# Sum of absolute differences by row: longer loads on one queue, the second half of y in the first half's place, and the absolute sums on ScalarE

## The chip, the cores and the metric

The kernel runs on one core of a Trainium2 chip (trn2). The metric is the device time of one execution in microseconds (us). Lower is better.

## The reference

`x` and `y` are float32 matrices of 1024 rows and 4096 columns. The result is one float32 number per row:

```python
def reference(x, y, axis):            # axis = -1
    return np.sum(np.abs(x - y), axis=axis).astype(np.float32)
```

Two matrices of 16.78 MB each are read, 33.55 MB in all, and 4 KB are written.

## The kernel before

The 128 partitions of the on-chip memory (SBUF) each take K = 8 neighbouring rows: partition p holds rows 8p to 8p + 7 (`"(p k) c -> p k c"`, L15 to L17). So one pass of the loop (L29) handles one row of every partition, a tile of 128 x 4096 elements with 16 KB per partition, 2 MB in all. There are eight passes, and each has four steps:

- L33: SyncE's queue (SP) loads the row of x into the tile `tx`;
- L34: ScalarE's queue (ACTq) loads the row of y into the tile `ty`;
- L35: VectorE subtracts, `tx = tx - ty`, in place;
- L36: VectorE sums the absolute values of `tx` along the row into one column of `ro` (128 x 8).

After the loop SP stores `ro` (L38). ScalarE itself computes nothing; it only issues the loads of y.

`tx` and `ty` come from two pools of four buffers each (L23, L24). The first four passes therefore find free buffers, and a later load has to wait until its buffer has been read: the load of x for the reduction of four passes before, the load of y for the subtraction. The loads are written in program order, but the order of the operations on each engine is set by the framework's scheduler, not by the order in the source: the trace shows which order it chose. All waits (semaphores) are put in by the framework.

Of the kernel before, what the change touches and what calls it, by code (L numbers as in the profile page):

```python
# [5 lines left out]

KCS = [1]*8

@with_exitstack
def kernel(ctx, tc, x, y, axis, out):  # L10
    nc = tc.nc
    P = nc.NUM_PARTITIONS
    R, C = x.shape
    K = R // P
    xr = x.rearrange("(p k) c -> p k c", p=P, k=K)  # L15
    yr = y.rearrange("(p k) c -> p k c", p=P, k=K)
    orr = out.rearrange("(p k) -> p k", p=P, k=K)  # L17
    kcs = KCS
    assert sum(kcs) == K
    pools = {}  # L20
    for kc in set(kcs):
        pools[kc] = (
            ctx.enter_context(tc.tile_pool(name=f"px{kc}", bufs=4)),  # L23
            ctx.enter_context(tc.tile_pool(name=f"py{kc}", bufs=4)),  # L24
        )
    with tc.tile_pool(name="pr", bufs=1) as poolr:
        ro = poolr.tile([P, K], mybir.dt.float32)
        o = 0
        for kc in kcs:  # L29
            poolx, pooly = pools[kc]  # L30
            tx = poolx.tile([P, kc, C], x.dtype)
            ty = pooly.tile([P, kc, C], y.dtype)
            nc.sync.dma_start(out=tx, in_=xr[:, o:o+kc, :])  # L33
            nc.scalar.dma_start(out=ty, in_=yr[:, o:o+kc, :])  # L34
            nc.vector.tensor_sub(out=tx, in0=tx, in1=ty)  # L35
            nc.vector.reduce_sum(out=ro[:, o:o+kc], in_=tx, axis=mybir.AxisListType.X, apply_absolute_value=True)  # L36
            o += kc
        nc.sync.dma_start(out=orr, in_=ro)  # L38


# [1 line left out]
_INS = ['x', 'y', 'axis']  # L42
_OUTS = [((1024,), 'float32')]
#: Inputs that are plain numbers.
_NUMBERS = {'axis': -1}


def kernel(**inputs):
    import numpy as _np
    import concourse.bacc as _bacc  # L50
    import concourse.tile as _tile
    from concourse import mybir as _mybir
    from concourse.bass_utils import run_bass_kernel_spmd as _run

    nc = _bacc.Bacc("TRN2", target_bir_lowering=False, num_devices=1)  # L55
    arrays, args = {}, []
    for name in _INS:
        if name in _NUMBERS:
            args.append(_NUMBERS[name])
            continue  # L60
        a = _np.ascontiguousarray(inputs[name])
        if a.dtype.kind in "iu":
            a = a.astype(_np.int64)
        arrays[f"in_{name}_dram"] = a
        args.append(nc.dram_tensor(f"in_{name}_dram", a.shape, _mybir.dt.from_np(a.dtype), kind="ExternalInput").ap())
    for i, (shape, dtype) in enumerate(_OUTS):
        dt = _mybir.dt.from_np(_np.dtype(dtype))
        args.append(nc.dram_tensor(f"out_{i}_dram", shape, dt, kind="ExternalOutput").ap())
    with _tile.TileContext(nc) as tc:
        kernel(tc, *args)  # L70
    r = _run(nc, [arrays], core_ids=[0])
    got = tuple(r.results[0][f"out_{i}_dram"] for i in range(len(_OUTS)))
    return got[0]
```

## Time and profile before

| | |
|---|---|
| time, median of 3 runs | 97.6 us (97.56 to 97.62) |
| span of the profiled execution, first to last instruction | 95.8 us |
| VectorE (DVE) busy | 69.9 us, 73% of the span, 16 operations |
| ScalarE, TensorE, GpSimd | nothing, but for four small constants written by GpSimd |
| loads | 33.55 MB, mean 350 GB/s over the span |
| chain that ended last | DMA 68%, DVE 24%, issue 4%, ACTq 1% |

The runs give the time of an execution as a whole and the profile gives the span inside one, so the 1.8 us between 97.6 and 95.8 are what lies around the span. For the profiled execution no time but its span is shown.

How to read it: the page gives for each engine its busy time as a share of the span, and a strip of 40 equal slices of the span with the busy tenths in each. The chain is the work that ended last, followed backwards from the last instruction, at each step to whatever released it. A group of instructions is one line of the source on one engine: the tiles it writes and reads, the shapes, how often, the busy time, the mean of one, and the idle time just before it with what ended that. For a queue, the page gives the packets and bytes that it moved and the time that its packets took as a share of 16 transfer engines over the whole span. SPq and ACTq are the parts of SyncE and ScalarE that issue transfers.

### The profile page before, as it was taken

How to read it: one execution, taken by the hardware profiler on the slowest of the kernel's cores; microseconds unless marked ns; L12 is line 12 of the kernel's file. 1: busy time of each engine (PE TensorE's matmuls, PEld its weight loads, DVE VectorE, ACT ScalarE, POOL GpSimd, SP SyncE). 2: the span in 40 equal slices, each digit the busy share in tenths (PEclk: the TensorE clock that was granted, in tenths of full speed). 3: DMA queues.
4: the chain of work that ended last, by engine and by line, in shares of the span. 5: the costliest groups of instructions: out<-in, count | busy, mean ns of one | idle time of the engine just before them, and what ended most of it. 6: DMA issues, size and time to landing. Idle time of an engine off the chain costs nothing.

```text
span 95.8 us, 95 instructions
## 1 busy us (share of the span) xinstructions
DVE 69.9 (73%) x16; POOL 0.2 (0%) x4
## 2 busy tenths in 40 slices
DVE  0000069996930499999982999999909999999990
POOL 0000000000000000000000000000000000000000
DMA  4899999999999999999999999999999995000000
GB/s 109 369 431 424 424 438 438 438 431 438 431 424 438 424 417 431 431 411 431 438 438 424 431 431 431 424 424 424 431 411 438 438 438 212 0 0 0 0 0 2
DMA packets 2448, 33.56 MB, mean 350 GB/s; under 512 B 400, under 2 KB 400, under 8 KB 400
## 3 DMA queue, kind: packets, MB, share of 16 engines
q1 hardware_dynamic: 1296, 16.78, 41.7%
q10 hardware_dynamic: 1152, 16.78, 41.1%
HBM read 33.55 MB, written 0.00 MB: 350 GB/s over the span
## 4 chain that ended last, share of the span: by engine, by line
DMA 68%; DVE 24%; issue 4%; ACTq 1%
DMA ty<-in_y_dram 68%; DVE tx L35 14%; DVE ro L36 10%; ACTq L34 1%
## 5 line engine op out<-in xcount | busy, mean ns | idle before, releaser
L35 DVE TENSOR_TENSOR tx<-tx,ty 128x4096 f32<-128x4096 f32 x8 | 35.4, 4422 | 23.6 <-DMA ty<-in_y_dram 23.6
L36 DVE TENSOR_REDUCE ro<-tx 128x1 f32<-128x4096 f32 x8 | 35.1, 4413 | 0.1
L55 POOL MEMSET const-bfloat16-1.0<- 128x1 bf16 x1 | 0.1, 103 | 0.0
L55 POOL MEMSET const-uint8-127<- 128x1 uint8 x1 | 0.1, 103 | 0.0
L55 POOL MEMSET const-float32-1.0<- 128x1 f32 x1 | 0.1, 100 | 0.0
L55 POOL MEMSET const-float32-0.0<- 128x1 f32 x1 | 0.1, 99 | 0.2 <-issue 0.2
## 6 DMA issues: line engine op xcount, KB each, us to landing
ty<-in_y_dram ACTq DMA_DIRECT2D x8, 2048.0 KB, 33.1
tx<-in_x_dram SPq DMA_DIRECT2D x8, 2048.0 KB, 23.6
out_dram<-ro SPq DMA_DIRECT2D x1, 4.0 KB, 1.4
```

Source lines behind the costliest of these rows:

```text
L34: nc.scalar.dma_start(out=ty, in_=yr[:, o:o+kc, :])
L35: nc.vector.tensor_sub(out=tx, in0=tx, in1=ty)
L36: nc.vector.reduce_sum(out=ro[:, o:o+kc], in_=tx, axis=mybir.AxisListType.X, apply_absolute_value=True)
L55: nc = _bacc.Bacc("TRN2", target_bir_lowering=False, num_devices=1)
```

## The change

The program now works with four large tiles instead of the pools. `xa` holds the first four rows of x of each partition, `xb` the last four, and `yb` the four rows of y that are needed now; `last` is a small tile for the end. The order of instructions on each engine is that of the source (`tc.manual_schedule()`).

- All loads are issued by SP, on one queue. The first four rows of x and then of y are one load each, 64 KB per partition; then follow three rows of x (48 KB per partition).
- After the subtraction of row k of the first half, row 4 + k of y is loaded into the place of row k of y. For the last row, x and y come in four pieces of 2304, 1152, 512 and 128 columns, x and y in turn.
- VectorE only subtracts. ScalarE takes the absolute value and the sum along the row in one operation (`activation` with `accum_out`).
- The last row is worked off piece by piece. ScalarE writes the sums of the first three pieces into three columns of `last`; VectorE writes the difference of the fourth piece beside them and sums the absolute values of these 3 + 128 columns into the last column of `ro`.

```diff
-KCS = [1]*8
+F32 = mybir.dt.float32
+ABS = mybir.ActivationFunctionType.Abs
+AX = mybir.AxisListType.X
+
+PIECES = [2304, 1152, 512, 128]
...
+    n_part = len(PIECES) - 1
+    H = K // 2
+    ps = ctx.enter_context(tc.tile_pool(name="ps", bufs=1))
+    with tc.manual_schedule():
+        xa = ps.tile([P, H, C], F32, tag="xa")
+        xb = ps.tile([P, H, C], F32, tag="xb")
+
+        yb = ps.tile([P, H, C], F32, tag="yb")
+        ro = ps.tile([P, K], F32, tag="ro")
+
+        last = ps.tile([P, n_part + PIECES[-1]], F32, tag="last")
+        nc.sync.dma_start(out=xa, in_=xr[:, 0:H, :])
+        nc.sync.dma_start(out=yb, in_=yr[:, 0:H, :])
+        nc.sync.dma_start(out=xb[:, 0:H - 1, :], in_=xr[:, H:K - 1, :])
+
+        def whole(tx, ty, k):
+            nc.vector.tensor_sub(out=tx, in0=tx, in1=ty)
+            nc.scalar.activation(tx, tx, ABS, accum_out=ro[:, k:k + 1])
+
+        for k in range(H):
+            whole(xa[:, k, :], yb[:, k, :], k)
+            if k < H - 1:
+                nc.sync.dma_start(out=yb[:, k, :], in_=yr[:, H + k, :])
+                continue
+            o = 0
+            for w in PIECES:
+                nc.sync.dma_start(out=xb[:, k, o:o + w], in_=xr[:, K - 1, o:o + w])
+                nc.sync.dma_start(out=yb[:, k, o:o + w], in_=yr[:, K - 1, o:o + w])
+                o += w
+        for k in range(H - 1):
+            whole(xb[:, k, :], yb[:, k, :], H + k)
+        tx, ty = xb[:, H - 1, :], yb[:, H - 1, :]
         o = 0
...
-            nc.sync.dma_start(out=tx, in_=xr[:, o:o+kc, :])
-            nc.scalar.dma_start(out=ty, in_=yr[:, o:o+kc, :])
-            nc.vector.tensor_sub(out=tx, in0=tx, in1=ty)
-            nc.vector.reduce_sum(out=ro[:, o:o+kc], in_=tx, axis=mybir.AxisListType.X, apply_absolute_value=True)
-            o += kc
+        for i, w in enumerate(PIECES):
+            s = slice(o, o + w)
+            if i < n_part:
+                nc.vector.tensor_sub(out=tx[:, s], in0=tx[:, s], in1=ty[:, s])
+                nc.scalar.activation(tx[:, s], tx[:, s], ABS, accum_out=last[:, i:i + 1])
+            else:
+                nc.vector.tensor_sub(out=last[:, n_part:n_part + w], in0=tx[:, s], in1=ty[:, s])
+                nc.vector.reduce_sum(out=ro[:, K - 1:K], in_=last, axis=AX, apply_absolute_value=True)
+            o += w
         nc.sync.dma_start(out=orr, in_=ro)
```

## Rows read from the trace of the kernel before

**Rows 1.** The page: the span, VectorE's busy time, and the transfers' share in 40 slices.

```profile
span 95.8 us, 95 instructions
...
DVE 69.9 (73%) x16; POOL 0.2 (0%) x4
...
DMA  4899999999999999999999999999999995000000
```

**Rows 2.** The chain of waits in order of time, its end: start, length, what.

```profile
36.97 34.71 DMA ty<-in_y_dram
71.68 0.02 issue
71.70 4.43 DVE tx L35
76.13 5.22 DVE ro L36 x2
81.34 3.36 issue
84.70 4.43 DVE tx L35
89.13 0.02 issue
89.15 4.42 DVE ro L36
```

**Rows 3.** The timeline of VectorE: start, length, operation, and the idle time before it.

```profile
12.92 4.43 DVE L35 TENSOR_TENSOR tx<-tx,ty 128x4096 f32<-128x4096 f32 x1 [12.92 <-DMA ty<-in_y_dram]
...
22.72 4.43 DVE L35 TENSOR_TENSOR tx<-tx,ty 128x4096 f32<-128x4096 f32 x1 [0.92 <-DMA ty<-in_y_dram]
32.51 4.43 DVE L35 TENSOR_TENSOR tx<-tx,ty 128x4096 f32<-128x4096 f32 x1 [5.37 <-DMA ty<-in_y_dram]
36.86 8.74 DVE L36 TENSOR_REDUCE ro<-tx 128x1 f32<-128x4096 f32 x2
...
76.04 8.74 DVE L36 TENSOR_REDUCE ro<-tx 128x1 f32<-128x4096 f32 x2
```

**Rows 4.** Stretches: busy time of DVE and POOL, clock, DMA share, GB/s (six between 12.9 and 71.7).

```profile
12.90:22.70 9.80, 8.85 (x2) 0.00 (x0) 1.00 1.01 431
...
32.50:42.30 9.80, 9.79 (x3) 0.00 (x0) 1.00 1.01 428
...
80.50:81.00 0.50, 0.50 (x1) 0.00 (x0) 1.00 0.02 0
```

**Rows 5.** The page: the two load queues, packets, MB, share of 16 engines.

```profile
q1 hardware_dynamic: 1296, 16.78, 41.7%
q10 hardware_dynamic: 1152, 16.78, 41.1%
```

**Rows 6.** The loads' issues (ns, minimum, median, maximum), and stretches at the start.

```profile
L34 ACTq DMA_DIRECT2D ty<-in_y_dram x8: 334/364/649, 0.7 to 50.0; - x8
...
L33 SPq DMA_DIRECT2D tx<-in_x_dram x8: 327/352/510, 0.7 to 60.9; - x8
...
0.73 1.88 SPq L33 DMA_DIRECT2D tx<-in_x_dram  x4
...
1.00:1.50 0.50, 0.00 (x0) 0.00 (x0) 1.00 0.00 0
1.50:2.00 0.50, 0.00 (x0) 0.00 (x0) 1.00 2.30 524
```

**Rows 7.** The waits of SP's queue: us in total, times, longest.

```profile
SPq L33 <- DVE ro L36: 46.5, 4, 18.7
```

**Rows 8.** The page: groups of instructions; busy us, mean ns of one, idle before.

```profile
L35 DVE TENSOR_TENSOR tx<-tx,ty 128x4096 f32<-128x4096 f32 x8 | 35.4, 4422 | 23.6 <-DMA ty<-in_y_dram 23.6
L36 DVE TENSOR_REDUCE ro<-tx 128x1 f32<-128x4096 f32 x8 | 35.1, 4413 | 0.1
...
L55 POOL MEMSET const-float32-1.0<- 128x1 f32 x1 | 0.1, 100 | 0.0
```

**Rows 9.** The timeline at the end: the store.

```profile
93.60 0.35 SPq L38 DMA_DIRECT2D out_dram<-ro  x1
```

**Rows 10.** Stretches around three places where the queues go from one load to the next.

```profile
11.30:12.90 1.60, 0.00 (x0) 0.00 (x0) 1.00 1.06 451
21.00:22.60 1.60, 0.80 (x1) 0.00 (x0) 1.00 1.06 451
30.80:32.40 1.60, 0.00 (x0) 0.00 (x0) 1.00 1.07 451
```

15 lines of the change are left out of this document (1 added, 14 removed).

## The prediction

> **What bounds the kernel now.** I read the page first, then the chain of waits, then the work stage by stage, then VectorE's order of time. On the page VectorE is busy for 73% of the span and the transfers fill nine tenths of each slice from the third to the 33rd [rows 1]: neither is the bound throughout. The chain of waits tells them apart in time. Until 71.70 us it is the loads of y but for the start and one subtraction; from there to the end every piece is VectorE work (the piece called "issue" at 81.34 lies inside the reduction that lasts until 84.70) [rows 2]. So two stages. First, the stream: row pairs of 4.19 MB land 9.80 and 9.79 us apart [rows 3], at 428 to 431 GB/s with the transfer engines' share at 1.01, in every stretch between 12.9 and 71.7 us; after 80.50 us no packet of the loads starts [rows 4]. Second, a tail: VectorE passes its wait for the last row at 81.34 us and finishes at 89.15 + 4.42 = 93.57 us, 12.2 us later. It is late because its own order holds reductions back: at 32.51 us the third subtraction runs ahead of the second row's reduction, and from 36.86 us two reductions stand together; the same pair stands at 76.04 us, in front of the last row's subtraction [rows 2, 3]. The sum of VectorE's work isn't the trouble (70 of 96 us), its placing is.
>
> The time is the span of 95.8 us and 1.8 us around it, 97.6 us, the median of the runs; I keep the 1.8 us.
>
> **The change, part by part.**
>
> *The stream.* No byte is removed. Eight rows at 9.79 us each are 78.3 us, and the first pair was usable at 12.92 us [rows 3], so data is usable at 12.92 - 9.79 = 3.13 us plus 2.33 us per MB, that is 4.90 us for each 16 KB row of one input. The new order on SP's queue gives: first half of x and of y (eight such rows) at 42.3; three rows of x at 57.0; rows 4, 5 and 6 of y at 61.9, 66.8 and 71.7; the four pairs of pieces (2304, 1152, 512 and 128 of 4096 columns, each times 9.79 us) at 77.2, 79.9, 81.2 and 81.5 us.
>
> What one queue does to the rate, the trace doesn't show: both queues move half the bytes [rows 5]. Bounds: the 16 KB packets take 82.8% of 16 x 95.8 us, 0.62 us each, with nothing between them, since the share stays at 1.01; what four times longer runs could save lies within the spread of the stretches, 431 against 428 GB/s, 0.5 us over the stream, and the 64 smaller packets per engine of the last row could cost that again. A gain beyond this is unlikely because the engines show no idle time to win. I take zero, with half a microsecond either way and a rival below for more.
>
> *Issues and waits on SP.* Eight loads of y leave ScalarE's queue, and SP issues 14 loads in all, at 0.33 to 0.65 us each [rows 6]. Three go out at the start without a wait and carry the stream to 57.0 us. The load of row 4 of y waits for the subtraction of row 0, row 5 for that of row 1, row 6 for that of row 2, and the first piece of y for that of row 3; behind each wait stand all later loads and the store. Those subtractions end at 46.7, 51.2, 55.6 and 60.0 us (next part), and each load's turn in the stream comes 9 us or more after that: about 56.1 us for row 4, 61.0, 65.9 and 73.5 us for the first piece of y (the usable time of the load ahead, less at most 0.9 us, since after 80.50 nothing more starts and the wait passes at 81.34 [rows 2, 4]). The eight pieces need 8 x 0.35 = 2.8 us to issue from 60 us. Even the old kernel's SP stood waiting for VectorE 46.5 us in four waits [rows 7] without a dip in the stream [rows 4]. So I cost these waits at nothing; the cover is the queue's stock, and if it is gone each late load costs its lateness plus about 1 us from issue to first bytes (0.73 us to somewhere between 1.50 and 2.00) [rows 6].
>
> *VectorE.* Eight whole reductions go (35.1 us), and eight subtractions of 4.42 us stay [rows 8], the last cut in four. Starts wait for the first half to land at 42.3: subtractions end at 46.7, 51.2, 55.6, 60.0; then, each released by its y row, at 66.3, 71.2 and 76.1. Pieces by columns: 2.49, 1.24, 0.55 and 0.14 us (the smallest operation on the page takes 0.10 us [rows 8]), ending at 79.7, 81.2, 81.8 and 81.9.
>
> *ScalarE.* Nothing of it runs in the trace, so its price is bounded by neighbours. Low end: it keeps up with the data and costs no time of its own; then the closing reduction over 131 columns (0.15 us) ends at 82.1. Nearest row: VectorE's reduction of the same tile, absolute sum and all, 4.41 us for 4096 columns [rows 8]. I take that: row 6 runs from 76.1 to 80.5, and the pieces, queued behind it, add 2.48, 1.24 and 0.55 us: 84.8. ScalarE, not the stream, then sets the end. High end: half as much again, 6.6 us per row; row 6 ends at 82.7, the pieces at 89.1, the time is 93.3 us. Whatever ScalarE has to set up before its first operation has the 46 us before it for cover. In the Trainium skill, "ScalarE: Activation LUTs", What ACT_TABLE_LOAD costs, an activation with a pointer bias takes 280 ns and 0.833 ns per element; an estimate by that is 3.69 us per row, a last piece done at 83.9 and a time of 88.1 us; no run here shows it yet.
>
> *The tail.* After ScalarE's last piece the closing reduction takes 0.15 us: 85.0. Then the store as now: 93.60 to the span's end at 95.8 is 2.2 us behind VectorE's end [rows 1, 9]. Span 87.2 us, time **89.0 us**. The tail behind the last landing shrinks from 12.2 to 3.5 us, which is the whole gain.
>
> **Rivals.**
>
> *ScalarE is no bound.* It works row 6 off before the pieces need it, and the end follows the data: 82.1 + 2.2 + 1.8 = 86.1 us. For it: three of the four pieces are small. Against: it must be far under VectorE's own rate, and row 6 leaves it only 3.6 us between 76.1 and 79.7. Chance 8%, for anything under 87.0.
>
> *One queue leaves a few per cent.* Something between two packets of one queue that the other queue filled. 3% of 78.3 us is 2.4 us, time about 91.4; chance 11% for 91 to 97.
>
> *Slower: the seams between loads are bare.* Its place is the 13 seams between 14 loads in one queue. Its price: if the next load's first bytes only start once the load before has ended, about 1 us each, what the very first load takes from issue to bytes [rows 6]: 13 us, **102 us**. It decides from 8.6 / 13 = 0.66 us per seam on. For it: both queues were always stocked, so a seam in one could lie under the other. Against: both queues change loads together, x and y landing as a pair, and the stretches around these places (11.3 to 12.9, 21.0 to 22.6, 30.8 to 32.4 us) show 451 GB/s, no dip [rows 10]. Chance 4%. The Trainium skill, "DMA: Bandwidth & Descriptors", Anatomy of one DMA, speaks on this side with a fit that puts some 2.0 us of fixed cost into every transfer (measured for transfers issued from GpSimd); unhidden in the eight pieces alone that would be an estimated 16 us and a time near 105. The trace disagrees so far as loads in stock hide it [rows 10]; of pieces it shows nothing.
>
> *It doesn't do what it says.* The second half of y goes into a place whose other rows are still to be read. If the waits went by the whole buffer and not by the row, row 1's subtraction would wait for the load behind row 0's, to 61.9 us, and so on: subtractions at 61.9, 73.7 and 85.4 us (each 4.4 us of work, then 2.4 + 4.9 us of a bare load), the three others of the second half behind them from 89.8 to 103.1, the pieces another 5: about 112 us. Against: each wait names one row in the code. Chance 3%.
>
> **How the numbers follow.** The forecast holds 74%: 89.0 us, from 87.0 (ScalarE a fifth cheaper than VectorE, and half a microsecond of stream won) to 91.0 us (ScalarE a quarter dearer, or the stream 2 us longer). That range leaves out the four rivals and some edges, 2 in 10 at most, so it is the range. No change within 0.2%, about the smallest difference a measurement of this kernel can tell, has 1%; slower, the last two rivals less their lucky ends, 6%; faster 93%.
>
> **What would show it right or wrong.** Right: one queue with 33.5 MB at 425 GB/s or more and no dip until about 81 us; first subtraction near 42 us; VectorE idle between subtractions from 60 us on, released by y; ScalarE busy without a gap from 76 us, the closing reduction waiting for it; the chain of waits ending DMA, VectorE, ScalarE, VectorE. Wrong: SP's waits appearing as slices with a low transfer share around 56 to 75 us; the last landing later than 82 us; a gap in front of each piece; ScalarE's row far from 4.4 us (below 3.6 it is no bound, above 5.5 the time leaves the range); a subtraction released late by a load that was issued late.

## The result, and the profile after

The changed kernel takes 87.82 us (median of 4 runs, 87.69 to 87.86) against 97.61 us for the kernel before: a ratio of 0.8995, with a 95% interval of 0.8982 to 0.9008. The forecast was 89.0 us, between 87.0 and 91.0. The profiled execution took 87.86 us with a span of 86.1 us, so 1.8 us lie around it, as before.

First the page of the changed kernel: its span, the busy times, the transfers in 40 slices and the load queue. They answer to [rows 1, 5].

```profile
span 86.1 us, 104 instructions
...
DVE 35.8 (42%) x12; ACT 31.2 (36%) x21; POOL 0.2 (0%) x4
...
DMA  9199999768999999777998889899999999999400
...
q1 hardware_dynamic: 2160, 33.56, 92.0%
```

The transfers still last until about the same time: the strip falls in its 38th slice of 2.15 us, that is at about 81 us, where the strip of before fell in its 34th of 2.4 us. By the landings, the last load (64 KB of y, issued at 71.14 us) is there after 10.3 us, at 81.4 us; before, the last wait for a load passed at 81.34 us [rows 2]. What has gone is the long stretch without transfers behind it.

The sevens in the strip are no dip. They come from packets of 64 and 48 KB, which the views count where they start: between 19 and 20 us 16 packets of 64 KB start and take 2.42 us each, longer than a slice; between 18 and 19 us none starts. The rows land on time: the first half is usable at 41.99 us and row 4 at 61.43 us, 8.39 MB in 19.44 us or 431 GB/s. With 16 KB rows, below, the strip has nines in these places.

Then the end of the chain of waits, which answers to [rows 2]:

```profile
59.45 17.33 DMA yb<-in_y_dram
76.78 0.03 issue
76.81 0.02 DVEq L60
76.83 0.04 issue
76.88 2.57 DVE xb L60
79.45 0.02 issue
79.47 3.27 ACT xb L61 x3
82.74 0.09 ACTq L97
82.83 0.62 ACT xb L61 x2
83.45 0.02 issue
83.48 0.29 DVE ro L64
```

The chain runs DMA, VectorE, ScalarE, VectorE. It ends at 83.48 + 0.29 = 83.77 us; before, VectorE ended at 93.57 us [rows 2]. The difference is 9.80 us, and the times differ by 9.79 us. The last landing has hardly moved (81.34 and 81.4 us), so the whole gain lies behind it: from there to VectorE's end it was 12.2 us and is 2.4 us. The timeline of the same stretch shows who waited for whom (start, length, operation, idle time before it):

```profile
41.99 17.43 DVE L40 TENSOR_TENSOR xa<-xa,yb 128x4096 f32<-128x4096 f32 x4 [41.99 <-DMA yb<-in_y_dram]
46.45 9.00 SPq L46 DMA_DIRECT2D yb<-in_y_dram  x3
...
71.15 4.43 DVE L40 TENSOR_TENSOR xb<-xb,yb 128x4096 f32<-128x4096 f32 x1 [0.47 <-DMA yb<-in_y_dram]
...
75.61 3.62 ACT L41 ACTIVATE xb<-xb 128x4096 f32<-128x4096 f32 x1 [1.19 <-DVE xb L40]
76.88 2.56 DVE L60 TENSOR_TENSOR xb<-xb,yb 128x2304 f32<-128x2304 f32 x1 [1.30 <-DMA yb<-in_y_dram]
79.13 0.19 ACT L41 ACTIVATION_READ_ACCUMULATOR xb<-xb 128x1 f32 x1
79.47 2.12 ACT L61 ACTIVATE xb<-xb 128x2304 f32<-128x2304 f32 x1
79.74 2.08 DVE L60 TENSOR_TENSOR xb<-xb,yb 128x1152 f32<-128x1152 f32 x2 [0.30 <-DMA yb<-in_y_dram]
81.50 0.19 ACT L61 ACTIVATION_READ_ACCUMULATOR xb<-xb 128x1 f32 x1
81.59 1.15 ACT L61 ACTIVATE xb<-xb 128x1152 f32<-128x1152 f32 x1
81.74 0.28 DVE L63 TENSOR_TENSOR last<-xb,yb 128x128 f32<-128x128 f32 x1
82.65 0.19 ACT L61 ACTIVATION_READ_ACCUMULATOR xb<-xb 128x1 f32 x1
82.74 0.61 ACT L61 ACTIVATE xb<-xb 128x512 f32<-128x512 f32 x1
83.26 0.18 ACT L61 ACTIVATION_READ_ACCUMULATOR xb<-xb 128x1 f32 x1
83.48 0.29 DVE L64 TENSOR_REDUCE ro<-last 128x1 f32<-128x131 f32 x1 [1.45 <-ACT xb L61]
```

The first two rows are the start of VectorE's work, when the first half has landed, and SP's loads of rows 4 to 6 of y. At the end, VectorE waits for data before the first two pieces (1.30 and 0.30 us) and for nothing before the others. It has its last difference at 82.02 us and then waits 1.45 us for ScalarE. ScalarE works without a gap from 79.47 us on: three pieces and their read-outs, 4.0 us.

### The profile page after: what moved, and what is told of

Same layout as the page of the kernel before. It is cut to its first block, busy times and chain, and to the rows that moved or that the text cites. A ratio compares the mean times of both kernels' runs of the same rounds, so it can differ in the third digit from the quotient of the medians.

```text
span 86.1 us, 104 instructions
## 1 busy us (share of the span) xinstructions
DVE 35.8 (42%) x12; ACT 31.2 (36%) x21; POOL 0.2 (0%) x4
## 4 chain that ended last, share of the span: by engine, by line
DMA 67%; DVE 24%; ACT 5%; SPq 0%; issue 0%; ACTq 0%; DVEq 0%
DMA yb<-in_y_dram 67%; DVE xa L40 20%; ACT xb L61 5%; DVE xb L60 3%; SPq L35 0%; DVE ro L64 0%; ACTq L97 0%; DVEq L60 0%; DVEq L40 0%
## 5 line engine op out<-in xcount | busy, mean ns | idle before, releaser
L40 DVE TENSOR_TENSOR xa<-xa,yb 128x4096 f32<-128x4096 f32 x4 | 17.4, 4420 | 42.0 <-DMA yb<-in_y_dram 42.0
L41 ACT ACTIVATE xa<-xa 128x4096 f32<-128x4096 f32 x4 | 14.5, 3616 | 24.4 <-DVE xa L40 24.4
L40 DVE TENSOR_TENSOR xb<-xb,yb 128x4096 f32<-128x4096 f32 x3 | 13.3, 4426 | 2.9 <-DMA yb<-in_y_dram 2.9
L41 ACT ACTIVATE xb<-xb 128x4096 f32<-128x4096 f32 x3 | 10.8, 3616 | 5.0 <-DVE xb L40 5.0
L41 ACT ACT_TABLE_LOAD x1 | 1.3, 1283 | 22.6 <-DMA xa<-in_x_dram 22.6
L60 DVE TENSOR_TENSOR xb<-xb,yb 128x2304 f32<-128x2304 f32 (+2 forms) x3 | 4.6, 1537 | 1.6 <-DMA yb<-in_y_dram 1.6
L61 ACT ACTIVATE xb<-xb 128x2304 f32<-128x2304 f32 (+2 forms) x3 | 3.9, 1294 | 0.1
L41 ACT ACTIVATION_READ_ACCUMULATOR xa<-xa 128x1 f32 x4 | 0.7, 186 | 0.0
L41 ACT ACTIVATION_READ_ACCUMULATOR xb<-xb 128x1 f32 x3 | 0.6, 186 | 0.0
L61 ACT ACTIVATION_READ_ACCUMULATOR xb<-xb 128x1 f32 x3 | 0.6, 186 | 0.0
```

The source lines that it names most:

```text
L41: nc.scalar.activation(tx, tx, ABS, accum_out=ro[:, k:k + 1])
L60: nc.vector.tensor_sub(out=tx[:, s], in0=tx[:, s], in1=ty[:, s])
L61: nc.scalar.activation(tx[:, s], tx[:, s], ABS, accum_out=last[:, i:i + 1])
```

## The experiments

Each ratio is to the kernel before as measured together with it (97.58 to 97.64 us).

| kernel | time, us (median) | ratio to before, 95% interval |
|---|---|---|
| the changed kernel | 87.82 | 0.8995 (0.8982 to 0.9008) |
| before, in the order of the source | 94.47 | 0.9675 (0.9661 to 0.9690) |
| that, with the last row in pieces | 94.31 | 0.9672 (0.9656 to 0.9688) |
| order of the source, sums on ScalarE | 93.68 | 0.9592 (0.9577 to 0.9606) |
| changed, last row whole | 93.21 | 0.9549 (0.9533 to 0.9565) |
| changed, first half of y on ScalarE's queue | 87.95 | 0.9007 (0.8994 to 0.9021) |
| changed, 16 KB rows throughout | 88.28 | 0.9037 (0.9026 to 0.9049) |
| changed, no load in stock | 104.08 | 1.0658 (1.0622 to 1.0694) |
| changed, one ScalarE operation twice | 89.18 | 0.9144 (0.9122 to 0.9166) |
| changed, sums on VectorE | 117.31 | 1.2010 (1.1955 to 1.2066) |
| changed, tail balanced anew | 86.93 | 0.8900 (0.8889 to 0.8912) |

My theory is that the gain is the shorter tail behind the last landing, and that the stream of loads neither gains nor loses. The main rivals are that the loads (long runs, one queue) or the relief of VectorE carry it.

**The order alone.**

```diff
-    with tc.tile_pool(name="pr", bufs=1) as poolr:
+    with tc.manual_schedule(), tc.tile_pool(name="pr", bufs=1) as poolr:
```

> The kernel before with one change: the instructions keep the order of the source, so each row's reduction stands right behind its subtraction. My theory (the gain is the shorter tail of work behind the last landing): the last wait passes at 81.34 us as before, then 4.42 + 4.41 us of VectorE end at 90.2, with 2.2 and 1.8 us behind it 94.2 us, 3.4 us less than before. Rival (VectorE's order is idle talk, the gain comes from the loads and from ScalarE): 97.6 us, unchanged.

Measured: 94.47 us. The timeline of its VectorE at the end:

```profile
71.69 4.43 DVE L35 TENSOR_TENSOR tx<-tx,ty 128x4096 f32<-128x4096 f32 x1 [0.92 <-DMA ty<-in_y_dram]
76.15 4.42 DVE L36 TENSOR_REDUCE ro<-tx 128x1 f32<-128x4096 f32 x1
81.47 4.43 DVE L35 TENSOR_TENSOR tx<-tx,ty 128x4096 f32<-128x4096 f32 x1 [0.90 <-DMA ty<-in_y_dram]
85.93 4.42 DVE L36 TENSOR_REDUCE ro<-tx 128x1 f32<-128x4096 f32 x1
```

VectorE now waits 0.9 us for every row: it keeps up with the stream, and the last row costs its own two operations only, 8.9 us. VectorE ends at 90.35 instead of 93.57 us, so the old order had cost about 3.2 us, the backlog of [rows 3].

**The order and ScalarE.** Beside the order of the source:

```diff
-            nc.scalar.dma_start(out=ty, in_=yr[:, o:o+kc, :])
+            nc.sync.dma_start(out=ty, in_=yr[:, o:o+kc, :])
...
-            nc.vector.reduce_sum(out=ro[:, o:o+kc], in_=tx, axis=mybir.AxisListType.X, apply_absolute_value=True)
+            nc.scalar.activation(tx[:, 0, :], tx[:, 0, :], mybir.ActivationFunctionType.Abs, accum_out=ro[:, o:o+kc])
```

> Order of the source, the absolute sums on ScalarE, and the loads of y moved to SP behind those of x, still 16 KB rows in rotating buffers and no pieces. My theory: stream as before, last wait at 81.3 us, subtraction to 85.8, then ScalarE's 3.62 + 0.1 us and no VectorE work behind it: 89.5, time 93.5 us. So ScalarE by itself is worth under 1 us beyond the order. Rival (relieving VectorE is what brings the gain): within 1 us of 87.8 us.

Measured: 93.68 us. Taking half of the work off VectorE brings 0.8 us over the order alone, about the difference between one row's reduction on VectorE (4.42 us) and on ScalarE (3.62 us). VectorE's relief as such is worth nothing, because the last row still passes through both engines one after the other: its subtraction on VectorE from 81.52 us, its sum on ScalarE from 85.98 to 89.60 us.

**The last row whole, in the changed kernel.** The loop over the pieces becomes one load of x and one of y, and the last row goes through the same two operations as the others.

> The changed kernel with the last row loaded and worked off whole, no pieces. My theory: the last wait passes at about 81.2 us, subtraction to 85.6, ScalarE to 89.3, time 89.3 + 2.3 + 1.8 = 93.4 us: the pieces are worth some 5.6 us. Rival (long loads and one queue carry the gain): within 0.5 us of 87.8 us.

Measured: 93.21 us, 5.4 us above the changed kernel. Long loads in the new places, one queue and ScalarE without the pieces come out 0.5 us below the run before. The subtraction of the last row starts at 81.02 us here and at 81.52 us there: the long loads bring the stream forward by half a microsecond.

**The pieces alone.** The kernel before in the order of the source, with the last row loaded and worked off in the four pieces; VectorE subtracts and sums each.

> The kernel before in the order of the source, with the last row in the four pieces of the changed kernel, and VectorE still taking the sums; 16 KB rows, two queues. My theory (pieces are worth little while VectorE does both, because row 6 holds it until 80.5 us): 80.5 us and the 9.2 us that the pieces and the close took on VectorE alone end at 89.7; with 2.2 and 1.8 us behind it 93.7 us, 0.8 us under the order alone (94.5). Rival (the pieces bring their 5 us by themselves): 89.0 us or less.

Measured: 94.31 us, 0.6 us above what I expected and 0.2 us under the order alone, with intervals that overlap: no gain that can be told. Its timeline of VectorE:

```profile
71.67 4.43 DVE L45 TENSOR_TENSOR tx<-tx,ty 128x4096 f32<-128x4096 f32 x1 [0.94 <-DMA ty<-in_y_dram]
76.13 4.42 DVE L46 TENSOR_REDUCE ro<-tx 128x1 f32<-128x4096 f32 x1
80.46 2.55 DVE L52 TENSOR_TENSOR tx<-tx,ty 128x2304 f32<-128x2304 f32 x1
...
89.80 0.29 DVE L56 TENSOR_REDUCE ro<-last 128x1 f32<-128x131 f32 x1
```

The first piece is there before 80.46 us (nothing is waited for), but VectorE is busy with row 6 until then and spends 9.6 us on the pieces, where I had put 9.2. So pieces and ScalarE need each other: over the order alone, ScalarE by itself brings 0.8 us, the pieces by themselves 0.2 us, and both, in the run with 16 KB rows below (which also has the new places), 6.2 us.

**Two queues instead of one.**

```diff
-        nc.sync.dma_start(out=yb, in_=yr[:, 0:H, :])
+        nc.scalar.dma_start(out=yb, in_=yr[:, 0:H, :])
```

> The changed kernel with the first 8 MB of y issued by ScalarE's queue instead of SP's, so that two queues feed the first half. My theory (the number of queues is worth nothing): 87.8 us, within 0.3. Rival (one queue loses at seams between loads, or two lose by mixing): a difference of 0.5 us or more, either way, showing in the landing of the first half, 41.9 us in the changed kernel.

Measured: 87.95 us; its interval overlaps that of the changed kernel. The first subtraction starts at 42.26 us instead of 41.99. The number of queues makes no difference here that can be told. The two runs in the order of the source say the same of the whole stream: over two queues the last subtraction starts at 81.47 us, and over one, with the sums on ScalarE, at 81.52 us.

**Short runs on the one queue.**

```diff
-        nc.sync.dma_start(out=xa, in_=xr[:, 0:H, :])
-        nc.sync.dma_start(out=yb, in_=yr[:, 0:H, :])
-        nc.sync.dma_start(out=xb[:, 0:H - 1, :], in_=xr[:, H:K - 1, :])
+        for k in range(H):
+            nc.sync.dma_start(out=xa[:, k, :], in_=xr[:, k, :])
+            nc.sync.dma_start(out=yb[:, k, :], in_=yr[:, k, :])
+        for k in range(H - 1):
+            nc.sync.dma_start(out=xb[:, k, :], in_=xr[:, H + k, :])
```

> The changed kernel with the three long loads cut into eleven of one 16 KB row each, on the same one queue, x and y in turn. My theory (run length matters little): 16 KB packets take 0.611 us against 2.418 / 4 = 0.6045 in runs of 64 KB, 1.1% of 25.2 MB, 0.6 us; time 88.4 us at most. Rival (seams between loads in one queue are bare): eight more seams at 0.66 us or more, 93 us or more.

Measured: 88.28 us. The long runs of 64 and 48 KB, which also make eight seams fewer, are worth 0.46 us. If all of it were the seams, one would cost 0.06 us, less than a tenth of the 0.66 us from which that rival decided. It falls.

**No load in stock.** The three rows of x that bridge SP's wait for the first subtraction are loaded after row 6 of y.

```diff
-        nc.sync.dma_start(out=xb[:, 0:H - 1, :], in_=xr[:, H:K - 1, :])
...
+            nc.sync.dma_start(out=xb[:, 0:H - 1, :], in_=xr[:, H:K - 1, :])
             o = 0
             for w in PIECES:
```

> The changed kernel with the load of three rows of x moved behind row 6 of y, so that no load is in stock while SP waits for the subtraction of row 0. My theory (that stock is what hides SP's waits): the stream is dry from 41.5 to about 47.4 us, all pieces land some 6 us later, at about 86.8, and rows 4 to 6 wait for x until 77.3 us, so that VectorE ends at about 95.5, ScalarE at 98.4; time 102.8 us. Rival (the waits cost nothing in any order): 87.8 us. A dry gap alone, without the pile of work behind it, would give 93.8 us.

Measured: 104.08 us, the median of two runs of 103.67 and 104.49 us; the trace is of the faster. First the stretches around the wait (length, busy time of DVE, ACT and POOL, clock, DMA share, GB/s), then the timeline with SP's loads of rows 4 to 6 of y and VectorE's subtractions of these rows:

```profile
40.00:41.50 1.50, 0.00 (x0) 0.00 (x0) 0.00 (x0) 1.00 0.01 0
41.50:46.30 4.80, 4.45 (x2) 0.00 (x0) 0.00 (x0) 1.00 0.00 0
46.30:46.80 0.50, 0.50 (x1) 0.49 (x1) 0.00 (x0) 1.00 0.00 0
46.80:47.30 0.50, 0.50 (x1) 0.50 (x1) 0.00 (x0) 1.00 0.73 164
```

```profile
46.30 9.00 SPq L45 DMA_DIRECT2D yb<-in_y_dram  x3
...
78.54 13.10 DVE L39 TENSOR_TENSOR xb<-xb,yb 128x4096 f32<-128x4096 f32 x3 [19.26 <-DMA xb<-in_x_dram]
```

The stream stands still until SP, released by the first subtraction, issues at 46.30 us, and the first bytes come between 46.80 and 47.30 us: up to the first bytes the price of a bare seam is the lateness and somewhat under 1 us, as the prediction put it. (The last packets of 64 KB started between 38 and 39 us and lasted 2.42 us, so the standstill begins at about 41 us.) Rows 4 to 6 then wait for x until 78.54 us, and VectorE's pile ends late. This landing of x, 1.2 us later than worked out, makes up the excess over my figure (0.9 us in the execution of the trace, 1.3 us by the median). It was lost before the rows of x: row 6 of y lands at 63.9 us, 1.3 us late, and x 14.6 us after it, the pace of a full stream. The start behind the gap is slow: a share of 0.73 moves 164 GB/s, or 225 GB/s at a full share, against 434 in the changed kernel between 22 and 41.5 us. What part of the 1.2 us that is was not tried.

**One ScalarE operation twice.**

```diff
                 nc.scalar.activation(tx[:, s], tx[:, s], ABS, accum_out=last[:, i:i + 1])
+                if i == 1:
+                    nc.scalar.activation(tx[:, s], tx[:, s], ABS, accum_out=last[:, i:i + 1])
```

> The changed kernel with the second piece's ScalarE operation (1152 columns, 1.15 us) done twice, the second time over its own result. My theory (ScalarE sets the end behind the last landing): 1.15 us longer, 88.95 us. Rival (the last landing sets the end and ScalarE is hidden): no change, 87.8 us.

Measured: 89.18 us, 1.36 us more than the changed kernel. The timeline:

```profile
82.63 0.19 ACT L61 ACTIVATION_READ_ACCUMULATOR xb<-xb 128x1 f32 x1
82.85 1.16 ACT L63 ACTIVATE xb<-xb 128x1152 f32<-128x1152 f32 x1
83.92 0.19 ACT L63 ACTIVATION_READ_ACCUMULATOR xb<-xb 128x1 f32 x1
84.01 0.61 ACT L61 ACTIVATE xb<-xb 128x512 f32<-128x512 f32 x1
```

In the traces the close comes 1.27 us later than in the changed kernel: the operation comes through in full, with 0.1 us more since the repeat begins after the whole read-out of the first. ScalarE sets the end.

**The sums on VectorE.** Both `activation` calls of the changed kernel become `reduce_sum` with absolute values on VectorE.

> The changed kernel with the absolute sums back on VectorE. My theory (the long loads hold all work back until 42 us, so VectorE alone no longer fits behind them): 41.99 + 8 x 8.84 us of subtractions and reductions, and about 0.6 us for the pieces' fixed costs and the close, ends at 113.3; time 117.4 us, slower than before. Rival (VectorE, busy 42% of the span in the changed kernel, has room for the 35 us and only the tail grows): 92 us or less.

Measured: 117.31 us, 20% slower than before. In the changed order VectorE's 42% is no reserve, since its idle time lies before the first half has landed at 42 us. Half of the stream's time is given away at the start, and only engines that each need less than half of a row pair's 9.79 us make up for it: subtraction and sum on VectorE take 8.84 us a row, subtraction alone takes 4.42 and the sum on ScalarE 3.62.

**The tail balanced anew.**

```diff
-PIECES = [2304, 1152, 512, 128]
+PIECES = [1024, 1024, 1024, 640, 256, 128]
...
+        half = ps.tile([P, 2], F32, tag="half")
+        k, m = H - 2, C // 2
+        for j in range(2):
+            h = slice(j * m, j * m + m)
+            nc.vector.tensor_sub(out=xb[:, k, h], in0=xb[:, k, h], in1=yb[:, k, h])
+            nc.scalar.activation(xb[:, k, h], xb[:, k, h], ABS, accum_out=half[:, j:j + 1])
```

The two sums of `half` are added on VectorE after the second piece, the differences of the last two pieces go into `last`, and one closing reduction takes 4 + 384 columns.

> The changed kernel, with row 6 worked off in two halves so that ScalarE is free 1.7 us earlier, the last row in six pieces (1024, 1024, 1024, 640, 256, 128), of which VectorE sums the last two itself. My theory (ScalarE's backlog of about 1.5 us behind the last landing is the rest that can be had): the closing reduction starts at 82.1 and ends at 82.7 instead of 83.8 us; time 86.7 us. Rival (more pieces cost the stream and the issues what they save): 87.8 us or more, the last landing at 81.9 us or later.

Measured: 86.93 us, 0.9 us less than the changed kernel, with intervals apart: the fastest of all these kernels. Its timeline at the end:

```profile
80.39 0.83 DVE L68 TENSOR_TENSOR xb<-xb,yb 128x640 f32<-128x640 f32 x1 [0.44 <-DMA yb<-in_y_dram]
...
81.25 0.74 ACT L69 ACTIVATE xb<-xb 128x640 f32<-128x640 f32 x1
81.89 0.18 ACT L69 ACTIVATION_READ_ACCUMULATOR xb<-xb 128x1 f32 x1
82.11 0.56 DVE L76 TENSOR_REDUCE ro<-last 128x1 f32<-128x388 f32 x1 [0.28 <-ACT xb L69]
```

VectorE now waits 0.28 us for ScalarE instead of 1.45 us, and the closing reduction ends at 82.67 instead of 83.77 us. The last load lands at 81.4 us here too, so the additional pieces cost the stream nothing that can be told.

## Why the prediction was right

- **The bound.** The tail behind the last landing was the thing to look at, and its shortening is the whole gain (VectorE's end 9.80 us earlier, the time 9.79 us). One reading in it was confirmed by itself: VectorE's order of operations had cost 3.2 us. Taken one after the other, the times go down by 3.1 us (order), 0.8 (sums on ScalarE), 0.5 (long loads) and 5.4 us (pieces). Each of these prices holds only beside the steps before it: the pieces without ScalarE brought 0.2 us.
- **The stream.** I took zero, with half a microsecond either way. By the rows of the timeline the first half was usable at 41.99 us (42.3 expected), row 6 of y at 71.15 (71.7) and the first piece at 76.88 (77.2): 0.3 to 0.5 us won. The run with 16 KB rows shows that this is the length of the runs and the seams, which it does not tell apart (41.99, 71.15 and 76.88 us become 42.38, 71.75 and 77.32); two queues instead of one change nothing. At the very end the lead is spent: the last piece lands at 81.4 us (81.5 expected), where the last row loaded whole was usable at 81.02 us. The small packets of the pieces cost 0.4 us again, as the prediction had allowed.
- **SP's waits.** Costed at nothing, with the stock in the queue as cover, and right: without that stock the kernel is slower than before. But the list of waits wasn't complete. The five longest waits of SP in the changed kernel (the first is the wait for the first half):

```profile
SPq L46 <- DMA yb<-in_y_dram: 39.8, 1, 39.8
SPq L46 <- DVE xa L40: 12.5, 3, 4.5
SPq L66 <- DVE ro L64: 9.8, 1, 9.8
SPq L51 <- DMA yb<-in_y_dram: 4.6, 1, 4.6
SPq L50 <- DMA yb<-in_y_dram: 4.5, 1, 4.5
```

  L50 and L51 load the pieces, and two of them waited for landings of y: the last piece of x went out at 66.24 us and that of y at 71.14 us, as rows 5 and 6 landed, though no data asks for it. They had some 8 us to spare, since the stream came to them only at about 80 us.
- **VectorE.** Subtractions as costed (4.42 us). The small operations were mis-sized, harmlessly: 0.69, 0.28 and 0.29 us for 512, 128 and 131 columns, where columns alone gave 0.55, 0.14 and 0.15.
- **ScalarE.** The mechanism was right, that ScalarE's pieces and not the stream set the end; the extra operation and the new balance both show it. The size was off: 4.41 us a row, taken from VectorE, is 3.62 us and a read-out of 0.19 that lies half under it:

```profile
L41 ACT ACTIVATE xb<-xb 128x4096 f32<-128x4096 f32 x3 | 10.8, 3616 | 5.0 <-DVE xb L40 5.0
L41 ACT ACT_TABLE_LOAD x1 | 1.3, 1283 | 22.6 <-DMA xa<-in_x_dram 22.6
...
L61 ACT ACTIVATION_READ_ACCUMULATOR xb<-xb 128x1 f32 x3 | 0.6, 186 | 0.0
```

  So row 6 is done at 79.3 instead of 80.5 us, the first piece waits for its subtraction (79.47) and not for row 6, and the close comes at 83.77 instead of 85.0 us. That is the 1.2 us between forecast and time, but not all of it is ScalarE's. With 16 KB rows, where the first piece came about as worked out (77.32 against 77.2 us), the close was at 84.21 us and the time 88.28 us: some 0.7 us are ScalarE's rate and 0.5 us the lead of the stream.

  An estimate by the figures of the Trainium skill, "ScalarE: Activation LUTs", What ACT_TABLE_LOAD costs, for a pointer bias was 88.1 us. The trace agrees with them to about 2% for a row, 3.62 us against an estimated 3.69, and in the columns, 0.84 ns each between 512 and 4096 columns against 0.833; the fixed part comes out smaller, 0.61 us for 512 columns against an estimated 0.71. The setup of 1.28 us, before ScalarE's first operation, lay at 22.6 us, under cover.
- **The range.** Its upper end rested on an error. It let a dearer ScalarE count from row 6 on, but ScalarE works off the rows one after the other from 46.7 us. Above about 4.9 us a row this backlog (46.7 us and seven rows) ends later than row 6 by itself (76.1 us and one row). A quarter dearer (5.5 us a row), the prediction's own steps give about 95 us and not 91.0, and with 6.6 us a row about 103 and not 93.3. That ScalarE was cheaper than VectorE's row, and not dearer, no row had told: on this side the range held by luck. The sign "below 3.6 it is no bound" was wrong too: at 3.62 us, almost at this edge, the first piece no longer waited for row 6, but VectorE still waited 1.45 us for ScalarE's pieces. And the four rivals have 26 chances in 100 together, not "2 in 10 at most".
- **The rivals.** The Trainium skill gives a fixed cost per transfer in "DMA: Bandwidth & Descriptors", Anatomy of one DMA, measured for transfers issued from GpSimd. No such cost adds up in SP's queue while it has loads in stock: 22 loads instead of 14 cost 0.46 us in all. The waits went by the row and not by the buffer: SP issued row 4 of y as the first subtraction ended, and the second subtraction followed at once. No run shows any of the few per cent that the second rival took from a single queue, and the first, ScalarE as no bound, falls with the operation done twice.

## What to carry to other kernels

Ask of a change what it does behind the last landing: engine time that overlaps the loads is worth nothing there, and the order on an engine decides how much of it is left over at the end. To shorten such a tail two things are needed together, small last pieces and engines that are free when those land; either alone brought 0.2 to 0.8 us here, and both 6.2 us. A load that reuses a place cost nothing here as long as other loads stood in the queue for longer than the wait lasted, so put the loads that wait for nothing in front of those that do.

## What the runs showed that I had not expected

- Two loads of pieces waited for landings of other loads to which no data ties them, 4.5 and 4.6 us. The traces tell which landing it is, that of the load issued eight places earlier: the thirteenth and fourteenth load went out as the fifth and sixth (rows 5 and 6 of y) landed. With 16 KB rows eight loads go out by 4.6 us and the ninth at 8.05 us, when the first has landed; without the stock the fourteenth waits 14.2 us for the sixth, the three rows of x. So in these three traces no more than eight loads were under way at a time, and the stock in front of a wait was at most that deep. What the framework shares between them was not tried.
- Fixed costs of small operations: about 0.15 us on VectorE beyond the columns, and on ScalarE 0.61 us for 512 columns, of which some 0.43 us are columns at 0.84 ns.
- In the kernel without stock, 1.2 us of the stream, lost in the first rows behind the gap. The first bytes there come slowly; whether that is all of it stays open.
